# A fourth pair of split weights in place of a fourth load buffer, and the way back placed between an expert's two products

## The chip, the cores and the metric

The kernel runs on one core of one Trainium2 chip. The metric is the device time of one execution in microseconds; the time shown is a median of several executions.

## The reference, cut to what matters

Two transformer blocks over 256 tokens of width 1024, in float32. The change lies in the first block's mixture of experts: 32 experts in four groups, each token goes to two of them.

```
g_sel  = argmax(xt @ w_rg + b_rg)                 # one of 4 groups
top2   = top_k(expert logits within the group)    # two of its 8 experts, with gates
h      = silu(xb @ w_g[e]) * (xb @ w_u[e])        # xb: tokens of expert e; 1024 -> 512, twice
y      = h @ w_d[e]                               # 512 -> 1024
out[token] += gate * y                            # the way back to the tokens
```

An expert has three weight matrices of 2 MB each (gate, up, down), 192 MB over all experts, and few tokens.

## The kernel before, in words

**Weights.** All large weights stream from HBM in an order that the class `Plan` writes down. Its unit is the piece, 128 partitions by up to 2048 float32 columns; two neighbouring pieces are one load of 2048 KB, issued from SP's queue by `fetch` (line 308) into a raw tile of 16 KB a partition. `prepare` splits each piece in two: ACT casts it into `wh` (float32r, line 336), DVE subtracts this from the raw piece into `wl` (line 337). A raw tile is free when the second of its pieces is split; a pair `wh`, `wl` (8 KB a partition each) is free when the last product that reads it is done. Products then take both parts, which keeps nearly full precision.

**Buffers.** There are `R_W` = 3 pairs for the whole kernel. There are `R_RAW` = 2 raw tiles, and `widen` (line 364) adds one for the stages `cross` and `moe` and a second for `moe`, so the experts have four. When the next load belongs to a later stage, `fetch_more` drops the added ones.

**Order.** `piece` hands out the next split pair. Before that `ahead` (line 348) prepares pieces up to two places beyond the one wanted, and before each of these `fetch_more` issues every load for which a raw tile is listed as free. So loads, casts and subtractions stand in the queues in the order of use, some way ahead of the products.

**The experts** (`moe`, the loop from line 1225). Blocks hold two experts. For step `e` of 34 the program writes: `up(e)`, the products with the gate and the up weights, 16 with `wh` and 16 with `wl` (lines 1153, 1154), two pieces for each matrix, each matrix followed by a scaled copy out of PSUM on ACT (`eg`, line 1158); `down(e - 2)`, 8 + 8 products with the two down pieces (lines 1185, 1186), and after the second expert of a block a scaled copy `y` on ACT (line 1189); at every second step `act()`, which folds, applies silu and splits the hidden values (lines 1165 to 1173) that `down` of the next two steps reads. In between, `go` advances a generator that gathers and transposes the tokens of coming groups (`prep`: lines 1109, 1111, 1128, 1131).

The **way back** is `spread` (lines 1139 to 1144): for one half of the columns and one half of the tokens, one product per gathered block (up to three blocks) into one PSUM tile, and an addition to `x` on DVE. When three blocks are gathered, `down` puts four such items on the list `todo`, and each step takes at most one of them off, after `down` and `act`. At step 33, before the last `down`, whatever is left is flushed.

Instructions of one engine run in the order of its queue. The framework that builds the program may put them there in another order than they are written in, as long as data dependencies hold.

Of the kernel before, what the change touches and what calls it, by code (L numbers as in the profile page):

```python
# [9 lines left out]
F32R = mybir.dt.float32r  # L10
# [7 lines left out]
P = 128  # L18
# [8 lines left out]
R_W = 3  # L27
# [211 lines left out]
class Net:  # L239
    def __init__(self, ctx, tc, io, plan):  # L240
        self.tc, self.nc, self.io = tc, tc.nc, io
        nc = self.nc
        self.uid = 0
        self.rel = None
        self.nrm, self.nxt, self.after = None, None, None
        self.plan, self.starts, self.at, self.prepared, self.fetched, self.done = plan, plan.starts, 0, 0, 0, {}
        self.cp = ctx.enter_context(tc.tile_pool(name="cst", bufs=1, side="right"))
        self.rawp = ctx.enter_context(tc.tile_pool(name="raw", bufs=R_RAW, side="right"))
        self.held, self.rows = None, None
        self.free, self.raws, self.more = [self.rawp] * R_RAW, {}, []  # L250
        self.sm = ctx.enter_context(tc.tile_pool(name="sm", bufs=2, side="right"))
        self.xtp = ctx.enter_context(tc.tile_pool(name="xt", bufs=1))
        self.whp = ctx.enter_context(tc.tile_pool(name="wh", bufs=R_W))
        self.wlp = ctx.enter_context(tc.tile_pool(name="wl", bufs=R_W))
        self.ps = ctx.enter_context(tc.tile_pool(name="ps", bufs=2, space=PSUM))
        self.x = self.cp.tile([P, NT, D], F32, name="x")
        p0 = self.cp.tile([P, sum(w for _, w in PACK0)], F32, name="pack0")
        nc.scalar.dma_start(p0, io["pack0"])
        for t in range(NT):
            nc.sync.dma_start(self.x[:, t], io["x"][t * P:(t + 1) * P])  # L260
        self.fetch_more()
        p1 = self.cp.tile([P, sum(w for _, w in PACK1)], F32, name="pack1")
        nc.sync.dma_start(p1, io["pack1"])
        p2 = self.cp.tile([P, sum(w for _, w in PACK2)], F32, name="pack2")
        nc.sync.dma_start(p2, io["pack2"])
        self.v = v = {}
        for pk, pt in ((PACK0, p0), (PACK1, p1), (PACK2, p2)):
            o = 0
            for name, w in pk:
                v[name] = pt[:, o:o + w]  # L270
                o += w
        self.ident, self.vecT, self.causal, self.distm = v["ident"], v["vecT"], v["causal"], v["distm"]
        self.sink, self.bg = v["sink"], v["bg"]
        self.tri = v["tri"].rearrange("p (a j) -> p a j", a=3)
        self.ones = self.cp.tile([P, P], F32, name="ones")
        nc.vector.memset(self.ones, 1.0)
# [38 lines left out]
    def prepare(self, i):  # L315

        kk, n, _, pair = self.plan.pieces[i]
        pool, raw = self.raws.pop(i)
        if self.plan.load_of.get(i + 1) != self.plan.load_of[i]:
            self.free.append(pool)  # L320
        hi = self.whp.tile([P, 2048], F32R, name=self.n("wh"), tag="wh")
        lo = self.wlp.tile([P, 2048], F32R, name=self.n("wl"), tag="wl")
        h = hi[:, :kk * n].rearrange("p (k n) -> p k n", k=kk)
        l = lo[:, :kk * n].rearrange("p (k n) -> p k n", k=kk)
        if pair:
            for g in range(2):
                rv = raw[:, :, g * P:(g + 1) * P].rearrange("p k (j c) -> p k j c", j=2)
                hv = h.rearrange("p k (j g c) -> p k j g c", j=2, g=2)[:, :, :, g]
                lv = l.rearrange("p k (j g c) -> p k j g c", j=2, g=2)[:, :, :, g]
                self.nc.scalar.copy(hv, rv)  # L330
                self.nc.vector.tensor_tensor(lv, rv, hv.bitcast(F32), ALU.subtract)  # L331
        else:
            d = -(-kk // 4) if i in self.starts else kk
            for k in range(0, kk, d):
                ks = slice(k, min(k + d, kk))
                self.nc.scalar.copy(h[:, ks], raw[:, ks])  # L336
                self.nc.vector.tensor_tensor(l[:, ks], raw[:, ks], h[:, ks].bitcast(F32), ALU.subtract)  # L337
        self.done[i] = (h, l)
# [7 lines left out]
        return self.done.pop(i)  # L346

    def ahead(self, i):
        while self.prepared <= min(i + R_W - 1, len(self.plan.pieces) - 1):
            self.fetch_more()  # L350
            self.prepare(self.prepared)
            self.prepared += 1
# [628 lines left out]
    def moe(self, norm2=None):  # L981
        nc, io = self.nc, self.io
        with self.tc.tile_pool(name="moe", bufs=1) as pool:
# [153 lines left out]
            back, todo = [], []  # L1137

            def spread(blocks, hf, t):
                cs = slice(hf * 512, hf * 512 + 512)  # L1140
                pu = self.ptr()
                for n, (ST, y) in enumerate(blocks):
                    nc.tensor.matmul(pu, ST[:, t * P:(t + 1) * P], y[:, hf], start=n == 0, stop=n == len(blocks) - 1)
                nc.vector.tensor_tensor(self.x[:, t, cs], pu, self.x[:, t, cs], ALU.add)
# [77 lines left out]
            def go(n):  # L1222
                for _ in range(n):
                    next(gen, None)
            for e in range(NE + EPB):
                b, grp = e // EPB, e // GE
                if e < NE:
                    if e % GE == 0 and e + GE < NE:
                        gen = prep(grp + 1)
                    if e % EPB == 0:  # L1230
                        xb = st[grp][:, :, b % 2 * P:b % 2 * P + P]
                    up(e, 0, xb)
                    go(1)
                    up(e, 1, xb)
                    go(1)
                elif e == NE + 1:
                    while todo:
                        spread(*todo.pop(0))
                    if norm2 is not None:
                        self.norm2_start(pool, norm2)  # L1240
                if e >= EPB:
                    down(e - EPB)
                if e % EPB and e < NE:
                    act()
                if todo:
                    spread(*todo.pop(0))
                go(e % EPB)

    def overflow(self, pool, flag, xsh, xsl, rstd, Go):
# [322 lines left out]
def body(tc, io, out, plan, stages=STAGES):  # L1572
    with ExitStack() as ctx:
        net = Net(ctx, tc, io, plan)
        with ExitStack() as first, ExitStack() as more:
            for s, following in zip(stages, stages[1:] + (None,)):
                net.after = NORMS.get(following)
                if s == "mix":
                    net.keep = first.enter_context(tc.tile_pool(name="keep", bufs=1))
                    net.mix()  # L1580
                elif s == "cross":
                    if following == "moe":
                        net.held = more.enter_context(tc.tile_pool(name="held", bufs=1, side="right"))
                        net.widen(more)
                    net.cross()
                    first.close()
                elif s == "moe":
                    net.widen(more)
                    net.moe(0 if following == "fin1" else None)
                    more.close()  # L1590
                elif s == "f00":
                    net.ffn(0, 0, 0, "fin1" in stages,
                            ctx.enter_context(tc.tile_pool(name="rel", bufs=1, space=DRAM)) if following == "ma" else None)
                elif s == "ma":
                    net.mixer_a()
                elif s == "f01":
                    net.ffn(16, 0, 1)
                elif s == "f10":
                    net.ffn(24, 1, 0)
                elif s == "mb":  # L1600
                    net.mixer_b()
                elif s == "f11":
                    net.ffn(40, 1, 1, last=(io["final_g_2"], out) if following == "fin2" else None)
        if stages[-1] != "fin2":
            for t in range(NT):
                tc.nc.sync.dma_start(out[t * P:(t + 1) * P], net.x[:, t])
# [35 lines left out]
```

## Time and profile before

| | |
|---|---|
| median of 3 runs | 1864.03 us (1863.67 to 1864.69) |
| the profiled execution | 1864.27 us, span 1862.5 us |
| mean granted TensorE clock | 0.985 of full speed |
| busy in the span | PE 1796.6 us (96%), weight loads 1475.0 (79%), DVE 1295.9 (70%), ACT 1089.0 (58%) |
| read from HBM | 436.05 MB, 236 GB/s over the span |
| chain that ended last | PE 46%, DMA 2%, DVE 1% |
| loads of the experts | 96 of 2048 KB, median 10.0 us from issue to landing |

Matmuls are pipelined and their ends are modelled, so PE's busy share overstates how near it is to its peak. A group of instructions has, beside its busy time, the idle time of its engine just before it and what ended that wait. An engine called SPq is the queue from which the loads are issued; a load's flight is the time from issue to landing.

### The profile page before, as it was taken

How to read it: one execution, taken by the hardware profiler on the slowest of the kernel's cores; microseconds unless marked ns; L12 is line 12 of the kernel's file. 1: busy time of each engine (PE TensorE's matmuls, PEld its weight loads, DVE VectorE, ACT ScalarE, POOL GpSimd, SP SyncE). 2: the span in 40 equal slices, each digit the busy share in tenths (PEclk: the TensorE clock that was granted, in tenths of full speed). 3: DMA queues.
4: the chain of work that ended last, by engine and by line, in shares of the span. 5: the costliest groups of instructions: out<-in, count | busy, mean ns of one | idle time of the engine just before them, and what ended most of it. 6: DMA issues, size and time to landing. Idle time of an engine off the chain costs nothing. (4 is left out here: it accounts for less than half of the span.)

```text
span 1862.5 us, 22219 instructions
## 1 busy us (share of the span) xinstructions
PE 1796.6 (96%) x8776; PEld 1475.0 (79%) x8776; DVE 1295.9 (70%) x1727; ACT 1089.0 (58%) x1381; POOL 26.5 (1%) x42
## 2 busy tenths in 40 slices
PE   8999799999999999999999999999999899999998
PEld 7888677777777776788889888888888788888886
DVE  5987699898998998755487655555554679565554
ACT  5755598887988887544344554445444444355443
POOL 1000000000000000000000000000000000000000
PEclk9999799999999999999989999999999999999999
DMA  7344499999999996554444445445544745454442
GB/s 266 125 159 192 146 389 402 394 373 381 388 388 384 397 394 278 196 195 181 184 171 163 157 186 192 172 176 202 192 176 175 283 154 186 175 215 181 181 180 92
DMA packets 34635, 438.64 MB, mean 236 GB/s; under 512 B 4016, under 2 KB 4288, under 8 KB 7264
## 3 DMA queue, kind: packets, MB, share of 16 engines
q1 hardware_dynamic: 31520, 424.86, 59.1%
q0 software_dynamic: 2576, 11.67, 1.8%
q8 instruction: 70, 1.15, 0.2%
q10 hardware_dynamic: 432, 0.66, 0.1%
q14 instruction: 37, 0.30, 0.0%
HBM read 436.05 MB, written 2.63 MB: 236 GB/s over the span
## 5 line engine op out<-in xcount | busy, mean ns | idle before, releaser
L337 DVE TENSOR_TENSOR wl<-raw,wh 128x512 fp32r<-128x512 f32 (+3 forms) x605 | 929.3, 1565 | 384.0 <-ACT wh L336 382.4
L336 ACT CAST wh<-raw 128x512 fp32r<-128x512 f32 (+3 forms) x605 | 780.0, 1324 | 455.0 <-PE acc L375 330.8
L373 PE MATMUL acc<-wh,xh 128*128 128x512 f32 x912 | 362.5, 397 | 3.2 <-DVE zz L1475 2.4
L374 PE MATMUL acc<-wl,xh 128*128 128x512 f32 x912 | 357.9, 392 | 0.0
L375 PE MATMUL acc<-wh,xl 128*128 128x512 f32 x912 | 357.8, 392 | 0.0
L1154 PE MATMUL acc<-wl,xb 128*128 128x512 f32 x512 | 214.9, 420 | 20.4 <-DVE wl L337 18.8
L1153 PE MATMUL acc<-wh,xb 128*128 128x512 f32 x512 | 208.2, 407 | 0.7 <-ACTq L1252 0.7
L373 PEld LDWEIGHTS acc<-wh,xh 128*128 128x128 f32 x912 | 171.8, 188 | 38.4 <-issue 3.3
L375 PEld LDWEIGHTS acc<-wh,xl 128*128 128x128 f32 x912 | 171.6, 188 | 36.2 <-issue 0.5
L374 PEld LDWEIGHTS acc<-wl,xh 128*128 128x128 f32 x912 | 171.9, 188 | 34.3 <-issue 0.5
L1154 PEld LDWEIGHTS acc<-wl,xb 128*128 128x128 f32 x512 | 98.0, 191 | 58.3 <-DVE wl L337 39.0
L373 PE MATMUL acc<-wh,hhi 128*128 128x512 f32 x352 | 137.6, 391 | 0.0
L375 PE MATMUL acc<-wh,hlo 128*128 128x512 f32 x352 | 137.0, 389 | 0.0
L374 PE MATMUL acc<-wl,hhi 128*128 128x512 f32 x352 | 137.0, 389 | 0.0
L1153 PEld LDWEIGHTS acc<-wh,xb 128*128 128x128 f32 x512 | 98.5, 192 | 19.3 <-issue 1.2
L373 PE MATMUL acc<-xh,wh 128*128 128x256 f32 x352 | 103.2, 295 | 2.9 <-ACT wh L330 2.9
L1186 PE MATMUL pmi<-wl,eh 128*128 128x512 f32 x256 | 101.3, 433 | 4.6 <-DVE wl L337 4.1
L374 PE MATMUL acc<-xl,wh 128*128 128x256 f32 x352 | 103.0, 293 | 0.0
L375 PE MATMUL acc<-xh,wl 128*128 128x256 f32 x352 | 102.1, 291 | 0.4 <-DVE wl L331 0.4
L1185 PE MATMUL pmi<-wh,eh 128*128 128x512 f32 x256 | 96.2, 412 | 1.0 <-DVE eh L1173 0.8
L663 ACT ACTIVATE sg<-acc,rs_o 128x256 f32<-128x256 f32 x66 | 31.3, 475 | 94.0 <-PE acc L375 93.9
L375 PEld LDWEIGHTS acc<-wh,hlo 128*128 128x128 f32 x352 | 66.0, 188 | 13.7
(404 smaller groups left out, 2250.8 us busy)
## 6 DMA issues: line engine op xcount, KB each, us to landing
raw<-in_w_moe_dram SPq DMA_DIRECT2D x96, 2048.0 KB, 10.0
raw<-in_w_f_dram SPq DMA_DIRECT2D x60, 2048.0 KB, 8.5
raw<-in_w_mb_dram SPq DMA_DIRECT2D x16, 1536.0 KB, 6.6
raw<-in_w_ma_dram SPq DMA_DIRECT2D x8, 2048.0 KB, 7.7
raw<-in_w_mix_dram SPq DMA_DIRECT2D x6, 2048.0 KB, 8.6
raw<-in_w_f_dram SPq DMA_DIRECT2D x8, 1536.0 KB, 6.5
raw<-in_w_mb_dram SPq DMA_DIRECT2D x6, 2048.0 KB, 9.3
raw<-in_w_cross_dram SPq DMA_DIRECT2D x3, 2048.0 KB, 7.6
```

Source lines behind the costliest of these rows:

```text
L336: self.nc.scalar.copy(h[:, ks], raw[:, ks])
L337: self.nc.vector.tensor_tensor(l[:, ks], raw[:, ks], h[:, ks].bitcast(F32), ALU.subtract)
L373: mm(ps, ah, bh, start=start, stop=False)
L374: mm(ps, ah, bl, start=False, stop=False)
L375: mm(ps, al, bh, start=False, stop=stop)
L663: nc.scalar.activation(sg, ps[:, :256], AF.Silu, scale=rstd[:, t:t + 1])
L1153: nc.tensor.matmul(ps, xb[:, kk], wh[:, k], start=kk == 0, stop=False)
L1154: nc.tensor.matmul(ps, xb[:, kk], wl[:, k], start=False, stop=kk == KD - 1)
L1185: nc.tensor.matmul(yb[hf], h[:, kk], wh[:, kk % 2, cs], start=first and kk == 0, stop=False)
L1186: nc.tensor.matmul(yb[hf], h[:, kk], wl[:, kk % 2, cs], start=False, stop=end and kk == 3)
```

## The change

The second `widen` goes, so the experts have three raw tiles. A pool named `fourth` with one `wh` and one `wl` tile takes its place. While it is set, `prepare` gives every fourth piece, beginning with the first that is prepared inside the stage, to that pool, and `ahead` prepares pieces up to three places beyond the one wanted. At step 33 it is set back to none. The one item of `todo` that a step takes off is now written ahead of `down` and `act`, behind `up` and the second `go(1)`; before, it stood behind both.

```diff
--- before.py
+++ after.py
@@ -246,6 +246,7 @@
         self.plan, self.starts, self.at, self.prepared, self.fetched, self.done = plan, plan.starts, 0, 0, 0, {}
         self.cp = ctx.enter_context(tc.tile_pool(name="cst", bufs=1, side="right"))
         self.rawp = ctx.enter_context(tc.tile_pool(name="raw", bufs=R_RAW, side="right"))
+        self.fourth, self.turn = None, -1
         self.held, self.rows = None, None
         self.free, self.raws, self.more = [self.rawp] * R_RAW, {}, []
         self.sm = ctx.enter_context(tc.tile_pool(name="sm", bufs=2, side="right"))
@@ -318,8 +319,13 @@
         pool, raw = self.raws.pop(i)
         if self.plan.load_of.get(i + 1) != self.plan.load_of[i]:
             self.free.append(pool)
-        hi = self.whp.tile([P, 2048], F32R, name=self.n("wh"), tag="wh")
-        lo = self.wlp.tile([P, 2048], F32R, name=self.n("wl"), tag="wl")
+        whp, wlp = self.whp, self.wlp
+        if self.fourth is not None:
+            self.turn = (self.turn + 1) % (R_W + 1)
+            if self.turn == 0:
+                whp = wlp = self.fourth
+        hi = whp.tile([P, 2048], F32R, name=self.n("wh"), tag="wh")
+        lo = wlp.tile([P, 2048], F32R, name=self.n("wl"), tag="wl")
         h = hi[:, :kk * n].rearrange("p (k n) -> p k n", k=kk)
         l = lo[:, :kk * n].rearrange("p (k n) -> p k n", k=kk)
         if pair:
@@ -346,7 +352,7 @@
         return self.done.pop(i)
 
     def ahead(self, i):
-        while self.prepared <= min(i + R_W - 1, len(self.plan.pieces) - 1):
+        while self.prepared <= min(i + R_W - (self.fourth is None), len(self.plan.pieces) - 1):
             self.fetch_more()
             self.prepare(self.prepared)
             self.prepared += 1
@@ -1234,16 +1240,17 @@
                     up(e, 1, xb)
                     go(1)
                 elif e == NE + 1:
+                    self.fourth = None
                     while todo:
                         spread(*todo.pop(0))
                     if norm2 is not None:
                         self.norm2_start(pool, norm2)
+                if todo:
+                    spread(*todo.pop(0))
                 if e >= EPB:
                     down(e - EPB)
                 if e % EPB and e < NE:
                     act()
-                if todo:
-                    spread(*todo.pop(0))
                 go(e % EPB)
 
     def overflow(self, pool, flag, xsh, xsl, rstd, Go):
@@ -1585,7 +1592,7 @@
                     net.cross()
                     first.close()
                 elif s == "moe":
-                    net.widen(more)
+                    net.fourth = more.enter_context(tc.tile_pool(name="fourth", bufs=1, side="right"))
                     net.moe(0 if following == "fin1" else None)
                     more.close()
                 elif s == "f00":
```

## Rows read from the trace of the kernel before

**Rows 1.** The page: the span in 40 slices of 46.6 us, the mean busy share of the 16 DMA engines in tenths and what they moved; and the row of its part on DMA issues (KB of one, median us from issue to landing) that belongs to the experts.

```profile
DMA  7344499999999996554444445445544745454442
GB/s 266 125 159 192 146 389 402 394 373 381 388 388 384 397 394 278 196 195 181 184 171 163 157 186 192 172 176 202 192 176 175 283 154 186 175 215 181 181 180 92
...
raw<-in_w_moe_dram SPq DMA_DIRECT2D x96, 2048.0 KB, 10.0
```

**Rows 2.** The window view, 230 to 700 us: length, busy us and instructions of PE, weight loads, DVE, ACT, POOL, then the granted clock, the DMA share and GB/s.

```profile
230.00:700.00 470.00, 443.92 (x2033) 340.05 (x2032) 422.18 (x317) 409.73 (x362) 0.55 (x1) 0.99 0.97 388
```

**Rows 3.** Groups by line, 230 to 700 us: busy us in all, mean ns of one, idle us of the engine just before them and what ended it.

```profile
L337 DVE TENSOR_TENSOR wl<-raw,wh 128x2048 fp32r<-128x2048 f32 (+1 forms) x176 | 394.6, 2278 | 25.3 <-ACT wh L336 24.8
L336 ACT CAST wh<-raw 128x2048 fp32r<-128x2048 f32 x176 | 331.0, 1908 | 24.4 <-PE pmi L1185 16.3 <-PE acc L1153 7.4
...
L1154 PEld LDWEIGHTS acc<-wl,xb 128*128 128x128 f32 x474 | 90.0, 190 | 54.7 <-DVE wl L337 37.0 <-issue 1.2
...
L1143 PE MATMUL ptr<-y,ST 128*128 128x512 f32 x96 | 47.4, 596 | 0.0
...
L1186 PEld LDWEIGHTS pmi<-wl,eh 128*128 128x128 f32 x224 | 39.8, 188 | 23.2 <-DVE wl L337 9.5 <-issue 7.9
...
L1143 PEld LDWEIGHTS ptr<-y,ST 128*128 128x128 f32 x96 | 17.8, 188 | 9.7 <-issue 6.0 <-ACT y L1189 1.2
...
L1144 DVE TENSOR_TENSOR x<-ptr,x 128x512 f32<-128x512 f32 x16 | 11.0, 687 | 8.5 <-PE ptr L1143 8.5
...
L1168 DVE TENSOR_TENSOR esg<-ptr,esg 128x256 f32<-128x256 f32 x15 | 6.3, 418 | 0.0
```

**Rows 4.** The view of the tile `raw`, 230 to 700 us: its loads; what ended the idle time before its readers (us, times), the whole list; and the time from issue to landing.

```profile
L308 SPq DMA_DIRECT2D raw<-in_w_moe_dram x88: 327/328/328, 230.3 to 699.5; - x88
...
  ACT wh L336: 24.8, 48
  PE pmi L1185: 16.3, 18
  PE acc L1153: 7.4, 14
...
DMA to landing us min/median/max: 7.6/10.1/12.7
```

**Rows 5.** The waits of the queue that issues the loads, 230 to 700 us: waited for, us in total, times, longest.

```profile
SPq L308 <- DVE wl L337: 344.7, 71, 7.7
```

**Rows 6.** The line that issues the loads, 224 to 709 us: count, ns min/median/max on the queue, first and last start in us.

```profile
L308 SPq DMA_DIRECT2D raw<-in_w_moe_dram x91: 327/328/332, 224.2 to 708.5; - x91
```

**Rows 7.** One load of the experts: its issue (351 to 352 us) and flight; then ACT and DVE in order of time from the casts of that load to its last subtraction (start us, us).

```profile
L308 SPq DMA_DIRECT2D raw<-in_w_moe_dram x1: 328/328/328, 351.4 to 351.4; - x1
...
DMA to landing us min/median/max: 10.2/10.2/10.2
...
367.26 1.94 ACT L336 CAST wh<-raw 128x2048 fp32r<-128x2048 f32 x1
...
369.37 1.93 ACT L336 CAST wh<-raw 128x2048 fp32r<-128x2048 f32 x1
...
369.23 2.29 DVE L337 TENSOR_TENSOR wl<-raw,wh 128x2048 fp32r<-128x2048 f32 x1 [1.01 <-ACT wh L336]
...
371.78 2.28 DVE L337 TENSOR_TENSOR wl<-raw,wh 128x2048 fp32r<-128x2048 f32 x1
```

**Rows 8.** The line that issues the loads in four short stretches, two loads in each: first and last start, and min/median/max from issue to landing.

```profile
L308 SPq DMA_DIRECT2D raw<-in_w_moe_dram x2: 327/328/328, 402.5 to 407.9; - x2
...
DMA to landing us min/median/max: 9.6/9.6/9.7
...
L308 SPq DMA_DIRECT2D raw<-in_w_moe_dram x2: 328/328/328, 451.0 to 457.3; - x2
...
DMA to landing us min/median/max: 8.9/9.5/10.1
...
L308 SPq DMA_DIRECT2D raw<-in_w_moe_dram x2: 328/328/328, 565.5 to 571.7; - x2
...
DMA to landing us min/median/max: 9.0/9.3/9.7
...
L308 SPq DMA_DIRECT2D raw<-in_w_moe_dram x2: 328/328/328, 599.3 to 604.5; - x2
...
DMA to landing us min/median/max: 8.5/9.2/9.9
```

**Rows 9.** The same for the first loads of the stage, 224 to 237 us.

```profile
L308 SPq DMA_DIRECT2D raw<-in_w_moe_dram x3: 327/328/332, 224.2 to 236.2; - x3
...
DMA to landing us min/median/max: 7.6/7.7/7.8
```

**Rows 10.** The same for three loads in a dense row, 521 to 532 us.

```profile
L308 SPq DMA_DIRECT2D raw<-in_w_moe_dram x3: 328/328/328, 521.1 to 531.1; - x3
...
DMA to landing us min/median/max: 12.3/12.5/12.7
```

**Rows 11.** Instructions in order of time around 332 us (start us, us).

```profile
332.06 0.40 PE L1153 MATMUL acc<-wh,xb 128*128 128x512 f32 x1
...
332.30 0.39 PE L1154 MATMUL acc<-wl,xb 128*128 128x512 f32 x1
...
332.55 1.12 PE L1143 MATMUL ptr<-y,ST 128*128 128x512 f32 x2
```

## The prediction

> **What bounds the kernel now.** I read the 40 slices first: from about 220 to 720 us the DMA row stands at its highest and the rate at twice that of the rest [rows 1]. That stretch is the experts, 96 loads of 2048 KB, and both edits lie in it. I then took the steady part of it, 230 to 700 us, and asked for four things.
>
> The window: PE is busy 444 of 470 us, DVE 422, ACT 410, and the DMA share is 0.97 [rows 2]. Nothing has room to spare, so busy time alone names no bound; the waits do.
>
> The groups by line: PE's weight loads stand 37.0 + 9.5 us before a `wl` that DVE hasn't finished; DVE stands 24.8 us before a `wh` from ACT; ACT stands 16.3 + 7.4 us until PE has let go of a pair [rows 3]. That is a loop round three split pairs, and its weakest member changes from piece to piece.
>
> The tile `raw`: among what ended the idle time before its readers there is no DMA at all [rows 4]. Every load had landed before ACT wanted it. The queue of the loads, for its part, stands until DVE's `wl` is done, which frees a raw buffer: 71 of its waits end so [rows 5]. So transfers are not the bound today, but they are paced by buffers, and the buffers are what the change touches.
>
> Last, the pace: 91 loads are issued between 224.2 and 708.5 us [rows 6], 484.3 / 90 = 5.38 us each; inside the window 470 / 88 = 5.34.
>
> **The life of a raw buffer.** One load, step by step [rows 7]: issued at 351.4, landed 10.2 us later at 361.6, first cast at 367.3, second subtraction ends at 371.78 + 2.28 = 374.1, and that is when the load four places on is issued. So 10.2 in flight, 5.7 lying ready, 6.8 being split, together 22.7. On average four buffers give 4 x 5.34 = 21.4 us; 10.1 of it is flight [rows 4]. The split cannot take less than one cast and two subtractions, 1.91 + 2 x 2.28 = 6.46 [rows 3]. That leaves 21.4 - 10.1 - 6.5 = 4.8 us in which a landed load lies ready or is interrupted. This cushion is what the fourth load buys.
>
> **The change, part by part.**
>
> *A raw buffer less.* With three, a load must go round in three periods. What is its flight then? Flight grows with what is already under way, so I looked at loads issued after a pause, where only the tail of one other was in flight: four pairs in mid-stage took 9.6 and 9.7, 8.9 and 10.1, 9.0 and 9.7, 8.5 and 9.9 us [rows 8], 9.4 on the mean, the second of each pair issued 2.6 to 4.7 us before the first had landed. That is the overlap three buffers would have: 9.5 of flight less a period of 5.5 is 4.0. The bounds: 7.7 us, for the three loads at the start that met hardly any other [rows 9], and today's median of 10.1. I take 9.5, by the eight, which have the spacing in question.
>
> From landing to free: 6.46 at least. DVE's other work is (422.2 - 394.6) / 88 = 0.31 us a load, ACT's (409.7 - 331.0) / 88 = 0.89 [rows 2, 3]; a starved ACT has about that much idle in each period, so I count 0.2 of it ahead of the first cast and all of DVE's: 7.0 together. The round is 9.5 + 7.0 = 16.5 us, the period 5.50. The break-even is 3 x 5.38 = 16.14. Bounds of the round: 7.7 + 6.46 = 14.2, at which buffers no longer bind, and 10.1 + 6.46 + 0.31 + 0.89 = 17.8, a period of 5.92. At 5.50 the 90 loads take 90 x (5.50 - 5.38) = **10.8 us more**.
>
> *A fourth split pair.* It lets ACT run one piece further ahead, and aims at the 23.7 us that ACT stands before PE and part of the 46.5 that PE stands before DVE [rows 3]. It pays only while raw data lie ready; if the round of the raw buffers sets the pace, PE's wait stays and only its cause moves back to the landing. So I cost it at zero while the buffers bind; without that, from zero to a gain held by the next floor: loads issued in a dense row, of 12.3 to 12.7 us flight, land (531.1 - 521.1) / 2 = 5.0 us apart, give or take 0.2 [rows 10], so 90 x (5.38 - 4.9) = 43 us at most. At the start one more piece can be split before the first product, worth up to one split, 2.5 us; I take 1.3.
>
> *The way back moved.* A `spread` is three products of two PE instructions each, 6 x 47.4 / 96 = 3.0 us, and one DVE addition of 0.69 [rows 3]. It issues no DMA and passes no queue but PE's and DVE's. It now stands ahead of the down product and of `act`. In front of the down product it gives DVE 3.0 us for the down pieces; behind it `act` comes 3.0 us later. Its chain, four instructions over ACT and DVE like the one of 0.42 us [rows 3], takes 1.7 and ends before the next expert's 32 up products do, 32 x 0.24 = 7.7 us by the spacing in the trace [rows 11]; without that cover 1.7 us in each of 16 pairs, 27 in all. What it can win: PE's 1.2 us before `y`, and DVE's 8.5 us before the sums [rows 3]; it can lose as much if the addition now stands in DVE's queue ahead of a subtraction. I take zero, between -9 and +9. The trace also shows that the place in the program isn't the place in the queue: at 332.55 the way back runs behind two products of the next expert, though it is written ahead of them [rows 11]. At the last expert three of them are flushed instead of two: 0 to 3.0 us, taken as 1.3, which cancels the start.
>
> *Putting `fourth` back to none at the last expert* costs nothing: all loads are issued by then.
>
> The sum is +10.8 us. The profiled execution took 1864.27 us (span 1862.5 and 1.8 around it), 0.24 above the median of 1864.03; against the latter I forecast **1875 us**.
>
> **The rivals.** A measurement of this kernel tells about 0.2%, 3.7 us, from no change.
>
> *Faster.* With the loads spaced evenly by three buffers, flight falls to the 7.7 us of the undisturbed ones [rows 9]. The round is then 14.7, a period of 4.9, the buffers don't bind, and the fourth pair takes the 23.7 us in which ACT stands before PE [rows 3]: 1864 - 24 = 1840. Against it: in mid-stage, even behind a pause, no load of the pairs took less than 8.5 [rows 8]. The Trainium skill, page "DMA: Bandwidth & Descriptors", section "Anatomy of one DMA", says that a transfer costs a fixed 2 us or so plus its bytes at 436 GB/s (measured there on GpSimd's path, not SP's); by that, as an estimate, a load flies 6.8 us and this rival wins. The trace agrees with the rate of that rule in the dense row (4.8 to 5.2 us apart) but not with its flight: 7.7 alone, 9.4 in mid-stage. Chance 0.24.
>
> *No change.* Interruptions fall into gaps that the starved engines have anyway; the round is 9.5 + 6.6 = 16.1, the period 5.38: 1864. PE waits as long as now, for the landing instead of the pair. Chance 0.12.
>
> *Much slower.* Casts never wait for a landing now [rows 4]. When they do, they stand at the head of ACT's queue, and the copies of `eg`, `xb` and `y` wait behind them, then PE, then the subtractions behind DVE's additions. All of ACT's and DVE's other work then lies in the round, with today's flight: 17.8 us, 5.92 a load, 90 x 0.54 = 49: 1913. This decides once a cast waits with a finished product queued behind it. Chance 0.10.
>
> The change does what it says as far as buffers go: two tiles of 8 KB a partition stand for one of 16 KB. Only the move may be undone by the order in which instructions are queued; that is in the bounds above.
>
> **How the numbers follow.** The forecast, a round of 16.3 to 17.2 us (5.43 to 5.73 a period, 1868 to 1896), has 0.54. Slower is 0.54 + 0.10 = 0.64, same 0.12, faster 0.24. Cases of both signs hold most of the chance, so the forecast's own range is 1868 to 1896; the range to hold 8 in 10 leaves out the much slower case and the better half of the faster one: 1847 to 1898.
>
> **What would show it.** In the same stretch of the changed kernel: loads 5.5 us apart with a median flight of 9.5; among the releasers of the casts the DMA of `raw`, which is missing now; the share of DMA under 0.97; hardly any wait of ACT for PE; PE's wait for `wl` at 50 us or more. I am wrong if flight falls under 9 us, if casts still find their data landed, or if the stage's pace goes under 5.3 us: then the fourth pair was worth more than the fourth load. If the pace is above 5.8, ACT's queue is the place to look.

## The result and the profile after

The changed kernel takes **1890.7 us** (median of 4 runs, 1887.7 to 1892.4) against 1864.4 for the one before on the same chip: a ratio of 1.0137, with a 95% interval of 1.0125 to 1.0149. The profiled execution took 1889.99 us, with a span of 1888.2, 25.7 more than the 1862.5 of before. The forecast was 11 us more; it was 26.

The same views in the same order. First the page: the slices of DMA and the row of the experts' loads, which answer to [rows 1].

```profile
DMA  6345399999999998554553345445445744455442
GB/s 261 125 157 195 123 351 372 366 363 380 375 355 376 373 398 335 204 212 178 187 216 135 121 189 194 176 178 208 183 167 198 267 182 177 179 200 190 178 172 96
...
raw<-in_w_moe_dram SPq DMA_DIRECT2D x96, 2048.0 KB, 9.7
```

The experts end one slice later, and while they last the rate stands at 351 to 380 GB/s in most slices, where it was 373 to 402. The loads fly a little shorter (9.7 for 10.0).

The window from 230 to 700 us (columns as in [rows 2]):

```profile
230.00:700.00 470.00, 437.22 (x1958) 335.16 (x1957) 401.36 (x306) 388.82 (x347) 0.55 (x1) 0.97 0.96 370
```

Every engine does less in the same 470 us: DVE 401 us for 422, ACT 389 for 410. The groups by line of that window, for [rows 3]:

```profile
L343 DVE TENSOR_TENSOR wl<-raw,wh 128x2048 fp32r<-128x2048 f32 (+1 forms) x167 | 374.3, 2277 | 42.8 <-ACT wh L342 42.6
L342 ACT CAST wh<-raw 128x2048 fp32r<-128x2048 f32 x166 | 309.5, 1904 | 41.9 <-DMA raw<-in_w_moe_dram 41.2
...
L1160 PEld LDWEIGHTS acc<-wl,xb 128*128 128x128 f32 x450 | 88.3, 196 | 59.1 <-DVE wl L343 39.2 <-issue 2.6
...
L1164 ACT ACTIVATE eg<-acc,gcol 64x512 f32<-64x512 f32 x57 | 38.9, 682 | 22.8 <-PE acc L1160 22.3
L1192 PEld LDWEIGHTS pmi<-wl,eh 128*128 128x128 f32 x216 | 38.3, 192 | 19.9 <-DVE wl L343 11.3 <-issue 2.9
...
L1150 DVE TENSOR_TENSOR x<-ptr,x 128x512 f32<-128x512 f32 x16 | 11.0, 686 | 5.6 <-PE ptr L1149 5.6
...
L1137 DVE SCALAR_TENSOR_TENSOR rjk<-ptr,pack 128x2 f32<-128x2 f32 x14 | 2.2, 159 | 19.7 <-PE ptr L1134 19.7
```

The loop round the split pairs is gone: in the window no cast waits for PE any more. In its place stand 41.2 us in which a cast waits for the DMA of `raw`, and DVE's wait for a cast has risen from 24.8 to 42.6. PE's wait for `wl` is 39.2 + 11.3 = 50.5, for 46.5. The tile `raw` says it directly, for [rows 4]:

```profile
L309 SPq DMA_DIRECT2D raw<-in_w_moe_dram x83: 327/328/332, 230.2 to 695.4; - x83
...
  ACT wh L342: 42.6, 46
  DMA raw<-in_w_moe_dram: 41.2, 40
...
DMA to landing us min/median/max: 7.6/9.7/11.2
```

The DMA, missing from this list before, ends 40 waits. The queue of the loads still stands before DVE's subtractions, as in [rows 5], with 362.5 us for 344.7:

```profile
SPq L309 <- DVE wl L343: 362.5, 68, 18.2
```

And the pace, the line that issues the loads, for [rows 6]:

```profile
L309 SPq DMA_DIRECT2D raw<-in_w_moe_dram x91: 327/328/332, 230.2 to 740.1; - x91
```

The 6th of the 96 loads is issued at 230.2 and the last at 740.1: 509.9 / 90 = 5.67 us each, for 5.38. That is 90 x 0.283 = 25.6 us, the whole difference of the spans. The row starts 6.0 us later than before and what follows its last load is 5.9 us shorter, as it must be when a load is issued three places ahead and not four.

**The round, measured.** I followed 81 loads of the steady part one by one, from issue to landing, to the first cast, to the end of the second subtraction, which frees the buffer. Means, in us:

| kernel | buffers | flight | landed to first cast | first cast to free | round | round / buffers | pace seen |
|---|---|---|---|---|---|---|---|
| before | 4 | 10.22 | 4.16 | 7.22 | 21.61 | 5.40 | 5.42 |
| after | 3 | 9.65 | 0.40 | 6.96 | 17.02 | 5.67 | 5.66 |
| forecast of after | 3 | 9.5 | 0.2 | 6.8 | 16.5 | 5.50 | |

The 4.2 us in which a landed load lay ready are spent, and the rest of the round is longer by 0.5 us than I had put it. What a landed load still waits for can be seen in one of them: the line of the loads from 343 to 347 us, and ACT in order of time from 351 to 360 us (start us, us; in brackets the idle time before and what ended it).

```profile
L309 SPq DMA_DIRECT2D raw<-in_w_moe_dram x1: 328/328/328, 345.3 to 345.3; - x1
...
DMA to landing us min/median/max: 8.2/8.2/8.2
```

```profile
349.57 3.71 ACT L342 CAST wh<-raw 128x2048 fp32r<-128x2048 f32 x2
355.24 0.68 ACT L1164 ACTIVATE eg<-acc,gcol 64x512 f32<-64x512 f32 x1 [1.96 <-PE acc L1160]
356.10 0.82 ACT L1117 CAST xb<-ptr 128x256 fp32r<-128x256 f32 x2 [0.18 <-PE ptr L1115]
356.81 3.71 ACT L342 CAST wh<-raw 128x2048 fp32r<-128x2048 f32 x2
```

This load was issued at 345.3 and landed 8.2 us later, at 353.5. Its first cast begins at 356.8. ACT stood 1.96 us at the head of its queue, at the copy of `eg` whose product PE was still making, then did `eg` and `xb`; the landed load lay behind them. Of the 81 loads 22 waited over 0.3 us for their first cast, and in 29 the first subtraction came late, behind other work of DVE or the subtraction of the piece before.

What the two engines did in these intervals can be added up from the trace. A round of after is some 0.9 us longer than its flight and one cast with two subtractions. Some 0.6 us of that is other work which lies ahead in ACT's or DVE's queue (`eg`, `xb`, the additions to `x`, the piece before); 0.23 us pass while ACT or DVE stands at an instruction that waits for PE (0.07 at `eg`, 0.11 at `rjk`); the rest lies between the end of one instruction and the start of the next. So of the 22.3 us that ACT stands before `eg` in the window, and of DVE's 19.7 before `rjk`, only some 6 and 9 us hold up a load that has landed.

### The profile page after: what moved, and what is told of

Read it like the earlier page. It is cut to its first block, busy times and chain, and to the rows that moved or that the text cites. A ratio compares the mean times of both kernels' runs of the same rounds, so it can differ in the third digit from the quotient of the medians.

```text
span 1888.2 us, 22122 instructions
## 1 busy us (share of the span) xinstructions
PE 1808.3 (96%) x8776; PEld 1484.3 (79%) x8776; DVE 1295.4 (69%) x1727; ACT 1088.9 (58%) x1381; POOL 26.8 (1%) x42
## 5 line engine op out<-in xcount | busy, mean ns | idle before, releaser
L1160 PE MATMUL acc<-wl,xb 128*128 128x512 f32 x512 | 222.3, 434 | 31.1 <-DVE wl L343 29.9
L1159 PE MATMUL acc<-wh,xb 128*128 128x512 f32 x512 | 212.7, 415 | 1.7 <-ACT wh L342 1.0
```

What stands on the lines that cost most here:

```text
L1159: nc.tensor.matmul(ps, xb[:, kk], wh[:, k], start=kk == 0, stop=False)
L1160: nc.tensor.matmul(ps, xb[:, kk], wl[:, k], start=False, stop=kk == KD - 1)
```

## The experiments

Theory A: with three raw buffers the round of a buffer sets the pace, which is round / 3, and neither the fourth pair nor the move changes it. Against it stood at first that the move or the fourth pair costs the time, and later that the order of ACT's queue does, whatever the buffers. A third rival is a limit of the rate at which transfers flow, whatever the number of buffers. Ratios are to the kernel before on the same chip, with 95% intervals.

**The parts one by one.** `third` takes only the fourth load away from the kernel before; `move` makes only the move; `unmoved` is the kernel after with the old place of the way back.

```diff
# third, against before
-                    net.widen(more)
                     net.moe(0 if following == "fin1" else None)
# move, against before (unmoved, against after: the reverse)
+                if todo:
+                    spread(*todo.pop(0))
                 if e >= EPB:
                     down(e - EPB)
...
-                if todo:
-                    spread(*todo.pop(0))
```

> The kernel before with the second added raw buffer taken away and nothing else: three raw buffers, three split pairs, the way back in its old place. Theory A, the round of a raw buffer sets the pace (flight 9.7, lying ready 0.6, split 6.8, divided by three buffers): the loads of the experts stand about 5.65 us apart as in the changed kernel, and the time is 1888 to 1893 us. Rival B, the fourth pair (its rotation, its extra look-ahead) or the move made it slow: 1862 to 1868 us. If the fourth pair had taken back part of a larger loss: above 1894.

> The kernel before with only the way back put ahead of the down product. Theory A: within 0.2% of before, 1861 to 1868 us, loads 5.38 us apart. Rival B, that the move is what costs: 1875 us or more.

> The changed kernel with the way back in its old place, so the buffers alone. Theory A: the time of the changed kernel, 1887 to 1894 us. Rival B, the move costs: under 1880. If the move helps while the buffers bind: above 1895.

`third` took 1892.8 us, 1.0152 [1.0135, 1.0169]; `move` 1864.4, 0.9994 [0.9984, 1.0003]; `unmoved` 1892.3, 1.0130 [1.0099, 1.0162]. All three lie where theory A put them. So the lost buffer alone costs all of it, the move nothing (though it does change the queues: the first addition to `x` starts at 341.3 us in `move` and at 333.8 in the kernel before), and the fourth pair wins back nothing that can be measured. The tile `raw` of `third`, 230 to 700 us:

```profile
L308 SPq DMA_DIRECT2D raw<-in_w_moe_dram x83: 327/328/328, 235.6 to 695.0; - x83
...
  DMA raw<-in_w_moe_dram: 44.8, 44
...
DMA to landing us min/median/max: 7.5/9.5/10.9
```

It is nearly the profile of after: 44.8 us of casts that wait for landings, a flight of 9.5; with three pairs casts stand 9.6 us before PE besides. Its round is 9.51 + 0.38 + 6.95 = 16.83 us, 5.61 by three, 5.60 seen.

**Another buffer less.** `two` leaves out both `widen` calls, so that two raw buffers are left, in the stage ahead of the experts too.

```diff
-                        net.widen(more)
                     net.cross()
...
-                    net.widen(more)
                     net.moe(0 if following == "fin1" else None)
```

> The kernel before with neither of the two added raw buffers: two raw buffers for cross and the experts, three pairs. Theory A, pace = round / number of buffers: with less overlap the flight is about 8.5, waiting 0.6, split 6.8, so 15.9 / 2 = 7.95 us a load, 90 x (7.95 - 5.38) = 231 us more, 2096 us; 2060 to 2130 with the flight between 7.7 and 9.3. Rival C, a limit of the transfers' rate that has nothing to do with the round: the same 1885 to 1900 as with three.

It took 2051.7 us, 1.1005 [1.0986, 1.1023], 44 less than I had worked out and under my range, but far from the 1885 to 1900 of a limit of the rate. The tile `raw` of `two`, 230 to 700 us:

```profile
L308 SPq DMA_DIRECT2D raw<-in_w_moe_dram x63: 327/328/328, 230.6 to 697.4; - x63
...
  DMA raw<-in_w_moe_dram: 101.7, 43
...
DMA to landing us min/median/max: 7.5/7.7/9.8
```

The law of theory A, pace = round / buffers, holds and its terms move: flight 7.80, since the load before is still in flight for only 0.8 us of it, 0.37 before the cast, 6.54 to be split, a round of 14.72 and 7.36 by two, which is the pace seen; 90 x (7.36 - 5.38) = 178 of the 191 us that the span is longer. I had carried the flight and the interruptions of three buffers over to two.

**A known delay in the round.** `plus_a` is the kernel after with one more copy of 128x256 on ACT right ahead of the first cast of every load of the experts; `plus_b` is the kernel before with the same.

```diff
+            if self.scratch is not None and self.plan.load_of.get(i - 1) != self.plan.load_of[i]:
+                self.nc.scalar.copy(self.scratch, raw[:, 0, 0:256])
             for k in range(0, kk, d):
```

> The changed kernel with one small ACT copy more for each load of the experts, 128x256 from the landed raw tile into a scratch tile, right ahead of the cast of its first piece: a known delay of about 0.38 us between landing and first cast. The order of the queues stays. Theory A, a delay enters the round one for one: the period grows by 0.38 / 3 = 0.13, 90 loads by 11 us, 1899 to 1904. Rival E, delays fill starved time: 1887 to 1894.

> The same copy put into the kernel before. There a landed load lies ready for 4.2 us before its cast. Theory A: the copy takes only ACT's time, which has some 0.7 us free in each period of 5.38; the raw round hides it and the loop of the split pairs feels a part: 1862 to 1870. If the copy costs here what it costs the changed kernel, 1873 or more, it is ACT's load and not the round that counts.

`plus_a` took 1900.2 us, 1.0196 [1.0179, 1.0213], some 9.5 more than the kernel after; `plus_b` 1870.0, 1.0031 [1.0021, 1.0041], 5.6 more than the kernel before. The groups of `plus_a` on ACT by line, 230 to 700 us:

```profile
L344 ACT CAST wh<-raw 128x2048 fp32r<-128x2048 f32 x164 | 306.0, 1904 | 0.0
...
L341 ACT COPY scratch<-raw 128x256 f32<-128x256 f32 x80 | 32.8, 410 | 37.8 <-DMA raw<-in_w_moe_dram 37.4
```

The copy takes 0.41 us and inherits the wait for the landing. The time from landing to first cast rises from 0.40 to 0.88, the round from 17.02 to 17.32: 30 rounds x 0.30 = 9 us. In the kernel before, the same copy costs 5.6 us, six tenths as much, though there 5.05 us lie between landing and first cast. So ACT's time has a price of its own beside the round, and how much of the 9.5 us in the kernel after is of that kind isn't shown. By the law a tenth of a microsecond in the round of after is worth 3 us, and this is the scale on which my forecast had to be right.

**The order of ACT's queue.** `after_q` holds the copies of `eg` and `y` behind the last cast written ahead of them, so that the fourth pair is really used as look-ahead. In the kernel as built it is not: counted in the order of ACT's queue, a copy of `eg` has three further pieces cast ahead of it in the first five copies, and two from there on, as it has in the kernel before.

```diff
+    def behind(self, ins):
+        # an order on ACT's queue, without a semaphore
+        self.tc.add_manual_dep(ins.ins, self.cast.name, ...)
...
-                nc.scalar.activation(st["gu", w][rows], ...)
+                self.behind(nc.scalar.activation(st["gu", w][rows], ...))
```

> The changed kernel with one thing pinned: on ACT's queue the copies eg and y stand behind the last cast that was written ahead of them. In the changed kernel's queue as built, only two further pieces are cast ahead of each copy eg from the sixth on, just as with three pairs, so the fourth pair is hardly used; pinned, it is three throughout. Theory A, the raw round binds: look-ahead that finds no landed load is worth nothing, 1884 to 1896 us, casts still waiting 40 us for landings. Theory D, the lost look-ahead is what the change fell short by: under 1872 us.

It took 1900.8 us, 1.0189 [1.0172, 1.0206]: slower than after, and 5 us over the range of theory A. The casts of `after_q`, 230 to 700 us (its profiled execution took 1912.4):

```profile
L342 ACT CAST wh<-raw 128x2048 fp32r<-128x2048 f32 x161 | 305.5, 1906 | 68.6 <-DMA raw<-in_w_moe_dram 59.8 <-DVE rpp L1110 3.3 <-DVE wl L343 2.8
```

The casts wait 59.8 us for landings in the window, for 41.2, and now `eg` stands behind casts that wait. Here a look-ahead over data that had not landed was worth nothing.

`nope` tries the opposite: it takes away what `eg` waits for. It leaves out the use of the experts' up products and of the gates: `eg` is copied from a constant, and so are the gates.

```diff
-                nc.scalar.activation(st["gu", w][rows], ps[rows], ...)
+                nc.scalar.activation(st["gu", w][rows]..., iota[rows]..., ...)
```

> The changed kernel with two waits for PE taken out of the queues that split the weights: the copy eg on ACT reads a constant instead of the up product, and gcol on DVE is made from a constant instead of a product (so gate and up products don't reach the output). All instructions stay. In the changed kernel a load waits 0.40 us for its cast and takes 6.97 from cast to free, where 0.2 and 6.77 were reckoned; ACT stands 22 us in eg, DVE 20 us in gcol, both before PE. Theory A: these waits are the missing part, since a landed load stands behind them; without them 0.2 + 6.6 + a flight of 9.65 = 16.45, 5.48 a load, 1874 us (1866 to 1881). Rival E: the waits only fill time in which ACT and DVE are starved anyway, or the flight grows by as much: 1885 or more.

It took 1907.5 us, 1.0239 [1.0216, 1.0263], and so went against what I expected. ACT in order of time from 418 to 431 us in `nope`:

```profile
418.45 3.74 ACT L342 CAST wh<-raw 128x2048 fp32r<-128x2048 f32 x2
422.86 0.38 ACT L1175 ACTIVATE esg<-ptr 128x256 f32<-128x256 f32 x1 [0.68 <-PE ptr L1173]
423.31 0.37 ACT L1117 CAST xb<-ptr 128x256 fp32r<-128x256 f32 x1
423.58 2.69 ACT L1164 ACTIVATE eg<-iota,gcol 64x512 f32<-64x512 f32 x4
426.29 3.70 ACT L342 CAST wh<-raw 128x2048 fp32r<-128x2048 f32 x2
```

With nothing to wait for, the queue was built in another order: four copies of `eg` in a row, 2.69 us. A load issued at 413.3 that landed 9.3 us later, at 422.6, is first cast at 426.3. On the mean landed to first cast is 1.61 us, flight 9.26 and the split 6.75, together 17.61; by three that is 5.87, the pace seen. So `nope` says nothing on what the wait at `eg` costs. What these waits cost by themselves no run shows.

**Half tiles.** `half_a` is the kernel after with six raw tiles of half the size, so that every piece has its own load of 1024 KB and is freed by its own subtraction, in all stages. `half_q` adds the order of `after_q`; `half_bq` is the kernel before with eight half tiles, three pairs and that order.

```diff
-        self.rawp = ctx.enter_context(tc.tile_pool(name="raw", bufs=R_RAW, side="right"))
+        self.rawp = ctx.enter_context(tc.tile_pool(name="raw", bufs=2 * R_RAW, side="right"))
...
-        raw = pool.tile([P, 4096], F32, name=self.n("raw"), tag="raw")
+                raw = pool.tile([P, 2048], F32, name=self.n("raw"), tag="raw")
...
-        if self.plan.load_of.get(i + 1) != self.plan.load_of[i]:
-            self.free.append(pool)
+        self.free.append(pool)
```

> The changed kernel with the same bytes of raw buffers cut in two: six tiles of 8 KB a partition, each filled by a transfer of one piece (1024 KB) and freed as soon as this piece is split. All stages load so. Theory A: a tile's round is a flight of 5 to 8 us and a split of 4.2 plus 0.9 of interruptions, 10 to 13 us, against six periods of 2.69 = 16.1, so the raw buffers no longer bind, casts hardly wait for a landing, and the fourth pair gets its chance: 1838 to 1864 us. Rival C, it is not the round but the rate at which the transfers can flow beside the engines: still 1885 us or more, with casts waiting for landings as long as in the changed kernel.

> The half tiles of half_a (six raw tiles of 8 KB a partition, transfers of 1024 KB in all stages, four pairs) with the same pinning. In half_a the queue had only one further piece cast ahead of most copies eg, and ACT stood 95 us in them before PE, so half_a was no test of the round. Pinned, it is three pieces. Theory A: a tile's round is a flight of 6.3 plus a split of 4.2 and about 1 of interruptions, 11.5 us against 16.1 at today's pace, so raw tiles do not bind and the time is 1838 to 1866. Rival C, transfers of this kind cannot flow faster beside the engines: 1885 or more with casts waiting for landings.

> The kernel before (three pairs, way back in its old place) with its raw buffers cut in two, eight tiles of 8 KB a partition with transfers of 1024 KB in all stages, and the copies eg and y pinned behind the last cast. Against half_q (1857 us) it has one split pair less and two half tiles more. If the fourth pair is worth something where raw tiles don't bind: 1863 to 1885. If not, 1851 to 1861.

`half_a` took 1935.1 us, 1.0370 [1.0353, 1.0387], against the 1838 to 1864 of theory A. It doesn't test the round, since the queue was built otherwise again; the waits of `half_a`, 230 to 700 us (waited for: us, times, longest):

```profile
DVE wl L344 <- ACT wh L343: 100.8, 53, 3.8
ACT eg L1165 <- PE acc L1161: 95.2, 40, 4.8
```

`eg` stands 95.2 us before PE, with one piece cast ahead of it in most places, and no cast waits for a landing. With the order pinned, `half_q` took **1857.2 us, 0.9961 [0.9946, 0.9975]**, faster than both kernels. Its tile `raw`, 230 to 700 us:

```profile
L314 SPq DMA_DIRECT2D raw<-in_w_moe_dram x174: 327/328/328, 231.5 to 699.4; - x174
...
  DMA raw<-in_w_moe_dram: 1.7, 2
...
DMA to landing us min/median/max: 4.9/7.4/10.0
```

Casts wait 1.7 us for landings in place of 41.2. `half_bq` took 1862.9, 0.9990 [0.9980, 0.9999], between the two ranges that I had given it. Where `half_q` gains can be read from one line, the additions of the way back to `x`: first and last start, in the kernel before, after, `half_q` and `half_bq`, in this order.

```profile
L1144 DVE TENSOR_TENSOR x<-ptr,x x24: 679/684/692, 333.8 to 746.3; 128x512 f32<-128x512 f32 x24
```

```profile
L1150 DVE TENSOR_TENSOR x<-ptr,x x24: 677/684/692, 351.8 to 773.9; 128x512 f32<-128x512 f32 x24
```

```profile
L1156 DVE TENSOR_TENSOR x<-ptr,x x24: 678/691/692, 342.3 to 751.2; 128x512 f32<-128x512 f32 x24
```

```profile
L1150 DVE TENSOR_TENSOR x<-ptr,x x24: 680/692/692, 337.3 to 758.4; 128x512 f32<-128x512 f32 x24
```

From the first up product (217.6, 220.3, 221.1 and 219.7 us) to the last of these additions the experts take 528.7, 553.6, 530.1 and 538.7 us. What follows in the span is 1116.2, 1114.3, 1105.2 and 1103.8. So smaller tiles, with the order held, give the experts back the 24.9 us that the lost buffer took, save 1.4; the net gain on before comes from the stages behind the experts, 11 to 12 us there. And with the raw buffers out of the way the fourth pair (with the move, which is worth nothing) takes 8.6 us off the experts, with two half tiles less.

**Where the raw buffers don't bind.** In `bytes_a` (the kernel after) and `bytes_b` (the kernel before) a load of the experts brings its first 1024 KB alone and both pieces are cast from them; half of the experts' weights are left out.

```diff
+        few = 2048 if key == "moe" else width
-        self.nc.sync.dma_start(raw[:, :width], ...)
+        self.nc.sync.dma_start(raw[:, :few], ...)
```

> The changed kernel in which each load of the experts brings only its first 1024 KB, and both of its pieces are cast from these: half of the expert weights are left out. Buffers, splits and products are as many as before; the queue keeps three pieces ahead. Theory A: flight falls to 5 to 6.3 us, the round to 13, under 3 x 5.38; the raw buffers do not bind, and the time shows what four pairs are worth without that limit: 1820 to 1862. If the round were not what binds: 1885 or more.

> The kernel before in which each load of the experts brings only its first 1024 KB and both pieces are cast from these (half of the expert weights are left out): four raw buffers and three pairs without a limit from the raw round. Against bytes_a (1831 us), with four pairs: the worth of the fourth pair alone where the raw buffers don't bind. By the forecast's price for it, 24 us, 1855 (1848 to 1862); worth nothing: 1827 to 1836.

`bytes_a` took 1830.9 us, 0.9817 [0.9797, 0.9837]; `bytes_b` 1838.9, 0.9858 [0.9833, 0.9882]. With a flight of 4.8 us for 9.7 the kernel after is 60 us faster. The queues were built otherwise here too: three or four pieces are cast ahead of each copy `eg` in `bytes_a`, and three ahead of most in `bytes_b`, where after and before have two. The order alone doesn't do it, since `after_q` with three pieces ahead and full loads took 1900.8; so the shorter load is what freed the kernel after. These two runs don't tell the flight from the bytes moved, but `half_q` moves all of the bytes, at 387 GB/s, and its casts don't wait for them either. The tile `raw` of `bytes_b`, 230 to 700 us:

```profile
L309 SPq DMA_DIRECT2D raw<-in_w_moe_dram x89: 327/328/328, 235.4 to 683.8; - x89
...
  PE acc L1154: 35.0, 26
...
DMA to landing us min/median/max: 4.6/4.8/9.6
```

The casts of `bytes_a` in the same window, with one pair more:

```profile
L343 ACT CAST wh<-raw 128x2048 fp32r<-128x2048 f32 (+1 forms) x194 | 353.0, 1856 | 27.5 <-PE acc L1160 8.5 <-PE pmi L1192 7.2 <-DMA raw<-in_w_f_dram 5.8
```

In `bytes_b` casts stand 35.0 us before PE until a pair is free; in `bytes_a` it is 8.5 + 7.2. That is what the fourth pair is for, and it is worth some 8 us (1838.9 - 1830.9; the intervals just touch), not the 24 that I had put on that wait. Why `bytes_b` is 25 us faster than the kernel before, in which no cast waits for a landing, is open: bytes and order changed together. Four raw buffers and four pairs together were not tried.

## Why the prediction was right in direction and wrong in size

- **What bounds.** Right: the three raw buffers, as `third` shows alone, with the waits for landings that the forecast asked for. The law, pace = round / buffers, held in every kernel in which the loads were followed one by one: 5.67 worked out and 5.66 seen for after, 5.61 and 5.60 for `third`, 7.36 and 7.36 for `two`, 5.87 and 5.87 for `nope`, 5.77 and 5.77 for `plus_a`. This by itself is bookkeeping, since each load is issued when a buffer comes free: it holds as well for the kernel before (5.40 and 5.42) and for `bytes_a` (4.98 and 5.01), where raw buffers don't bind. What tells the two apart is the time a landed load lies ready: 0.40 us in after, 4.16 in before, 2.8 in `bytes_a`.
- **The step that failed** is "the round is 9.5 + 7.0 = 16.5 us": it is 17.02. Flight is 0.15 longer; the wait ahead of the first cast 0.40 and not 0.2; from first cast to free 6.96 and not 6.8. Each is small, and 30 rounds x 0.52 = 15.6 us is the 15.7 us that I missed. I had counted 0.51 us of interruptions a round, ACT's 0.2 and DVE's 0.31; some 0.9 came. I had taken ACT's idle time in each period as room for most of its other work, but the work that stands ahead of a landed load in an engine's queue delays it even so. It is the greater part of the 0.9 us; the time in which ACT or DVE stands before PE is 0.23 of them. The kernel before had such waits as well, and its cushion hid them from the loads; `third` stands only 9.1 us before `eg` and loses as much as after (the lines stand below this list). The rival "much slower" had put all of that other work, 0.31 + 0.89 = 1.20 us, into the round: it had the mechanism, with too much of it and too long a flight.
- **The break-even** of 16.14 us made the forecast a small difference of two large numbers: 0.36 us a round was forecast, 0.88 came. An error of 3% in the round was one of 140% in the loss. My own bounds said so (16.3 to 17.2, 1868 to 1896), and the result lies within.
- **Flight** at 9.5 by the pairs behind a pause was near enough: 9.65, with 3.9 us of it beside the load before, for the 4.0 assumed. The Trainium skill, page "DMA: Bandwidth & Descriptors", section "Anatomy of one DMA", which spoke for the faster rival, gives some 6.8 us for such a load and 4.4 for half of it (estimates by 2 us and 436 GB/s, for another path of issue). By that the faster rival would have won; the runs come near it only where a load flies nearly alone, with 7.5 and 4.6 us as the shortest, and not in the steady stretch of after. Flight falls to 7.8 only in `two`, where the lost buffer costs more than it returns.
- **The fourth pair** costed at zero while buffers bind: right (`third` and after differ by 2 us, inside their intervals). Its price where they don't bind was too high: 24 us, for 6 to 8 in the two comparisons, each of which has another small difference beside the pair. The cap of 43 us on its gain went by landings 4.9 us apart, where the row has 5.0, which gives 34. With the fourth pair the other waits of the loop remain, and the queue as built looked further ahead for the first five copies of `eg` alone.
- **The move** at zero: right, 0.9994.
- **The start** at 1.3 us did not come: the split of the third load ends at 230.2, as before at 230.3, and the first up product starts later, at 220.3 us for 217.6. The flush is not told apart from the rest.
- **What would show it.** Flight, DMA among the releasers, a DMA share of 0.96, no wait of ACT's casts for PE, and PE's wait of 50.5 came as forecast; the pace of 5.67 stayed under the 5.8 from which I named ACT's queue, and that limit was too high.

The waits of ACT and DVE for PE, 230 to 700 us, in the kernel before (waited for: us, times, longest):

```profile
ACT eg L1158 <- PE acc L1154: 19.0, 31, 1.1
DVE rjk L1131 <- PE ptr L1128: 13.5, 8, 3.2
```

The same in `third`:

```profile
ACT eg L1158 <- PE acc L1154: 9.1, 15, 2.1
```

Open is what the time would be without one or another of these interruptions, since no run takes one out with the order of the queues held, and why half tiles help the stages behind the experts, where the loads were not followed.

## What to carry to other kernels

Before a load buffer is traded for something else, write the round of one buffer (flight, lying ready, being split) and divide it by the number left: if it comes within some per cent of the pace, every interruption of a landed load, by other work or by a wait that stands ahead of it in an engine's queue, counts once per round. A cushion of landed data is what pays for those interruptions, so take the interrupted round, not the shortest one, as the likely one. Where memory is short, the same bytes cut into more and smaller tiles, with the order of the queues held, gave back here what a whole buffer had taken; and after each such edit the order of the queue is to be read, since a buffer that the queue doesn't use is worth nothing.

## What the runs showed of the hardware

- In these runs flight follows the overlap with the load before: 7.80 us on the mean with 0.8 us of it (`two`), 9.65 with 3.9 (after), 10.22 with 4.8 (before). Loads of 1024 KB took 4.8 us in `bytes_a` and `bytes_b`, and 7.4 in `half_q`, where the DMA share is 0.99 at 387 GB/s.
- TensorE's granted clock, a mean over stretches at its two levels of 2.4 and 1.2 GHz, is 0.97 in the window of after and 0.99 in that of before. In `two` it is 0.90 over the same 470 us, with PE busy 371 of them for 444. It is no cause of the loss: `third` loses as much at 0.99.
